# VectorE's steps on adaLN's columns behind the low part of the last piece but one, and the last turned x kept next to the first eviction

## The chip, the cores and the metric

The kernel runs on one core of a Trainium2 chip. The metric is the device time of one execution in microseconds (us). Three runs of the kernel before took 906.33, 906.44 and 906.9 us; the median, 906.44 us, is the time before.

## The reference, cut to what matters

Batch 1, 256 tokens, D = 2048, E = 4096, all in float32:

```python
h = rmsnorm(x, norm_g)
mod = einsum('bd,df->bf', silu(c), ada_w) + ada_b     # 2048 x 6144 weights
shift, scale, gate = split(mod, 3)
h = h * (1 + scale) + shift
proj = einsum('bsd,de->bse', h, w_in)                 # 2048 x 16384 weights
b_gate, c_gate, v, g = split(proj, 4)
u = causal_depthwise_conv(c_gate * v, conv_w)         # width 3
y = b_gate * u * silu(g)
x = x + gate * einsum('bse,ed->bsd', y, w_out)        # 4096 x 2048 weights
out = rmsnorm(x, final_g)
```

The first product needs h, h needs adaLN's scale and shift, and these are themselves products with 2048 x 4096 weights. What this change concerns is how the kernel works on both kinds of weights at the same time.

## The kernel before, in words

**Products in three parts.** A float32 weight tile is loaded as `raw_s`, cast by ScalarE to float32r as its high part `hi` (L352, `split_hi`), and VectorE subtracts that from `raw_s` and gets the low part `lo` (L357, `split_lo`). The tokens are held in the same way: `hT` has for each block k of 128 features a high and a low half. TensorE multiplies high by high, high by low and low by high (L491, `product`): three products of 128x256 for each block k and each 128 columns. The tiles `raw`, `hi` and `lo` have three buffers each; a load of two blocks takes half a tile, so that two such loads share one.

**adaLN in groups.** The 16 blocks of features are made ready in eight groups of two (`ADA`). The first group is made in a prologue written in a fixed order. For each later group eight pieces of `ada_w` are loaded as tiles `at` (L460, two loads of 256 KB each, four buffers), and VectorE adds them up, each multiplied by silu(c): one step for each of 16 rows into `gv` (L472 for the first, L474 for the others, in `ada_sums`, which is traced at a lower priority by `GIVE`). When a group's 16 steps are done, TensorE transposes the sums (`tp_g`, L481), VectorE reduces them (L482) and adds the biases (`mod`, L324), ScalarE writes the high tokens (`hT`, L328) and VectorE the low tokens (L332, L335). Only then may TensorE use these two blocks k.

**Pieces of w_in.** Sixteen outputs (4 column chunks by 4 quarters) share the first part of the program. `plan()` makes a list of steps from a table of costs: a piece of `ada_w`, or the products of one output with the blocks that are ready by then (`part`). In its list the first 13 outputs take the first two blocks only, and the next three the first four; later they come again for the rest. Each part ends with an eviction from PSUM (`keep`: ScalarE copies it at L512, or VectorE adds at L514). PSUM has three buffers for these.

**What sets the order.** Python traces the steps in the plan's order, and a scheduler then sorts every engine's instructions by data dependencies, priorities and its own estimate of times. An engine runs what it is given in that order. `tc.add_manual_dep` with `after` adds an order between two instructions of one engine without a semaphore; `in_order` ties the prologue so, and `behind(ended)` puts instructions behind the prologue's last one on their engine. `keep_x(3, tp_3)` moves the last four transposed blocks of x from PSUM to `xs3` by four ScalarE instructions (L317); before, it is traced behind the second eviction (L574 to L577).

**Names.** Numbers in the order's rows are those of the program's buffers: `hi_376` and `lo_377` are the parts of `raw_s_375`, whose two halves are two outputs' first two blocks. `hi_444` and `lo_445` belong to `raw_s_443`, the next such tile. `raw_s_747` (`hi_748`, `lo_749`, PSUM `mm_s_746`) is the first piece with four blocks, two of which belong to the second group; `raw_s_812` (`hi_813`, `lo_814`, `mm_s_811`) is the next, and `mm_s_710`, evicted to `acc31`, is the output ahead of both, `mm_s_658` (`acc20`) the one ahead of that, `mm_s_878` the one behind.

Of the kernel before, what the change touches and what calls it, by code (L numbers as in the profile page):

```python
# [8 lines left out]
F32 = mybir.dt.float32  # L9
F32R = mybir.dt.float32r  # L10
AF = mybir.ActivationFunctionType
ALU = mybir.AluOpType
# [105 lines left out]
def short_conv_layer(ctx: ExitStack, tc: tile.TileContext, x, c, norm_g, ada_w, ada_b, w_in, conv_w, w_out, final_g, out):  # L118
    nc = tc.nc
# [43 lines left out]
    after = mybir.DependencyInfo(mybir.DependencyClass.NoSync, mybir.DependencyReason.DATA)  # L163
# [14 lines left out]
    @contextmanager  # L178
    def behind(last):

        traced = nc.cur_bb.bb.instructions
        n = len(traced)
        yield
        for ins in list(traced[n:]):
            if ins.engine in last:
                tc.add_manual_dep(ins, last[ins.engine], after, reason="behind")
# [13 lines left out]
    ended = {}  # L200
# [113 lines left out]
    def keep_x(j, tp):  # L314
        for i in range(CT):
            k = j * CT + i
            nc.scalar.activation(xs[j][:, i], tp[:, i], AF.Copy, scale=gT[:, k : k + 1])  # L317
# [19 lines left out]
    def modulate(k0, nk, sums):  # L337

        add_biases(k0, nk, sums)
        for k in range(k0, k0 + nk):  # L340
            high_tokens(k)
            low_tokens(k)

    def hi_tile():
        return w_tile("hi", "hi", F32R)

# [7 lines left out]

    def split_lo(raw, n, hi, lo_tag="lo", lo=None):
        lo = lo_tile(lo_tag) if lo is None else lo
        nc.vector.tensor_tensor(out=lo[:, :n], in0=raw[:, :n], in1=hi[:, :n].bitcast(F32), op=ALU.subtract)  # L357
        return hi, lo

    HALF = SLOT // 2  # L360
# [36 lines left out]
    for k in range(KT):  # L397
        c_k = silu_c[:, k : k + 1]
        at, gv = first_ada[k], gv0
# [47 lines left out]
    acc = {}  # L447
# [19 lines left out]
    def ada_sums(j, kk, at4, gv):  # L467
        for i in range(kk):
            c_k = silu_c[:, j + i : j + i + 1]
            if j + i == 0:  # L470
                with behind(ended):
                    nc.vector.tensor_scalar_mul(gv, at4[:, i], c_k)  # L472
            else:
                nc.vector.scalar_tensor_tensor(out=gv, in0=at4[:, i], scalar=c_k, in1=gv, op0=ALU.mult, op1=ALU.add)  # L474

    def ada_done(k0, nk, gv):

# [19 lines left out]
    def chunk_products(bank, hi, lo, o0, k, k0, k1, seed=False, late=False):  # L497


        begins = k == k0 and not seed  # L500
        terms = [(m, i) for i in (0, 2, 1) for m in range(CT)] if late else [(m, i) for m in range(CT) for i in range(3)]
        for m, i in terms:
            o = slice(o0 + m * P, o0 + (m + 1) * P)
            product(bank[:, m, :], hi[:, o], lo[:, o], k, i, begins and i == 0, m % 2 == 0, k == k1 - 1 and (m, i) == terms[-1])
# [3 lines left out]
    def keep(ch, q, k0, bank, seed=False):  # L508
        if k0 == 0 or seed:
            if k0 == 0:  # L510
                acc[ch, q] = slot([P, CT, T], f"acc{ch}{q}")
            nc.scalar.copy(acc[ch, q], bank)  # L512
        else:
            nc.vector.tensor_tensor(out=acc[ch, q], in0=bank, in1=acc[ch, q], op=ALU.add)  # L514

    def part(ch, q, k0, k1, seed):


        col = q * E + ch * CT * P
        step = SLOT // (CT * P)  # L520
        first = k0
        bank = psum.tile([P, CT, T], F32, tag="mm", name="mm_s")
        if seed:
            nc.scalar.copy(bank, acc[ch, q])
        if pieces0:
            for k in range(NK0):
                chunk_products(bank, *pieces0[k], 0, k, k0, k1, late=True)
            pieces0.clear()
            k0 = NK0
        for s0 in range(k0, k1, step):  # L530
            sk = min(step, k1 - s0)
            n = sk * CT * P
            raw, hi, lo = places(n)
            nc.sync.dma_start(
                raw[:, :n].rearrange("p (k f) -> p k f", k=sk),
                w_in[0, s0 * P : (s0 + sk) * P, col : col + CT * P].rearrange("(k p) f -> p k f", p=P),
            )
            with behind(ended if len(acc) < 3 else {}):
                split_lo(raw, n, split_hi(raw, n, hi), lo=lo)
            for i in range(sk):  # L540
                chunk_products(bank, hi, lo, i * CT * P, s0 + i, k0, k1, seed)
        keep(ch, q, first, bank, seed)

    ys = []
# [16 lines left out]
    for kind, *step in plan():  # L561
        if kind == "ada":
            ada_piece(*step)
        else:
            ch, k1 = step[0], step[3]
            part(*step)
            if step[2] == 0 and len(acc) in LATER:
                with tc.issue_after(last_mm[0].ins), behind(ended):
                    if len(acc) == LATER[0]:
                        rows2 = rows_tile("rows2")  # L570
                        nc.sync.dma_start(rows2[:, :], conv_w.rearrange("w (k p) -> (w k) p", p=P))
                    else:
                        turn(rows2, 0, 96, cw)
            if tp_3 is not None and len(acc) == 2:  # L574
                with behind(ended):
                    keep_x(3, tp_3)
                tp_3 = None  # L577
            whole[ch] += k1 == KT
            if k1 == KT and whole[ch] == 4:
                mixed(ch)  # L580
# [311 lines left out]
```

## Time and profile before

| | |
|---|---|
| median of three runs | 906.44 us |
| the profiled execution's own time | 906.58 us |
| its span, first to last instruction | 904.8 us |
| TensorE (PE) busy | 890.3 us, 98% |
| VectorE (DVE) busy | 665.8 us, 74% |
| ScalarE (ACT) busy | 477.8 us, 53% |
| mean granted TensorE clock | 0.998 |

How to read the rows that follow: in the timeline's rows stand the start in us, the duration in us (of all of a row's instructions together), the engine, the line in the kernel, the operation, what it writes from what, the shape, and how many instructions the row merges; in square brackets how long the engine stood idle before it, and what ended that. In the stages' rows stand the stretch, its length, each engine's busy time (and instructions) in the order PE, PEld (weight loads), DVE, ACT, POOL, then the granted clock, the DMA engines' share and GB/s. SP is the engine that issues the loads.

### The profile page before, as it was taken

The numbers are of one execution on the slowest core, as the hardware profiler recorded it, in microseconds if no ns is written. First come the engines' busy times: TensorE is split into PE (matmuls) and PEld (weight loads), VectorE is DVE, ScalarE is ACT, GpSimd is POOL, SyncE is SP. The second block draws the span as 40 slices with busy tenths as digits, with TensorE's granted clock in tenths as the row PEclk, the third lists the DMA queues.
The fourth block names the chain that finished last, engine by engine and source line by source line (L and its number), as shares of the span: only waits on it lengthen the run. The fifth ranks groups of instructions, "written<-read, shape, count | busy, mean of one in ns | idle before, by whom it ended". The sixth has DMA issues, their size and how long they took to land.

```text
span 904.8 us, 16390 instructions
## 1 busy us (share of the span) xinstructions
PE 890.3 (98%) x7009; PEld 852.8 (94%) x7009; DVE 665.8 (74%) x643; ACT 477.8 (53%) x423; POOL 87.3 (10%) x95
## 2 busy tenths in 40 slices
PE   7999999999999999999999999999999999999996
PEld 4899999999999999999999999999999988888885
DVE  5889989888888866766965677565555578887882
ACT  6768866665548766644433444443444445544342
POOL 0000000000000134024324103420000000000000
PEclk9999999999999999999999999999999999999999
DMA  9999999999998587688887888776566486685542
GB/s 313 365 372 366 361 304 349 362 369 347 355 323 289 164 278 242 189 258 244 281 251 237 255 271 266 231 228 191 187 190 195 135 313 197 224 281 187 186 139 94
DMA packets 162665, 235.00 MB, mean 260 GB/s; under 512 B 6804, under 2 KB 105284, under 8 KB 162208
## 3 DMA queue, kind: packets, MB, share of 16 engines
q1 hardware_dynamic: 159456, 226.56, 76.4%
q0 software_dynamic: 3008, 7.34, 2.9%
q8 instruction: 55, 0.90, 0.4%
q14 instruction: 18, 0.15, 0.0%
q10 hardware_dynamic: 128, 0.04, 0.0%
HBM read 224.49 MB, written 2.10 MB: 250 GB/s over the span
## 4 chain that ended last, share of the span: by engine, by line
PE 94%; DMA 3%; SPq 1%; DVE 1%; issue 1%; ACT 0%; ACTq 0%; DVEq 0%
PE mm_b L491 38%; PE mm_s L491 36%; PE mm_o L724 10%; PE mm_w L724 7%; DMA at<-in_ada_w_dram 2%; PE mm L724 2%; SPq L231 1%; DMA x<-in_x_dram 1%; DVE lo L357 0%; PE tp_g L481 0%; ACT hi L352 0%; DVE gv L474 0%; DVE hT L335 0%; ACT big L817 0%; ACT z L866 0%
## 5 line engine op out<-in xcount | busy, mean ns | idle before, releaser
L491 PE MATMUL mm_s<-hT,hi 128*128 128x256 f32 x2048 | 350.0, 277 | 1.0 <-ACT hT L328 1.0
L491 PE MATMUL mm_b<-hT,hi 128*128 128x256 f32 x2048 | 348.2, 276 | 0.0
L491 PEld LDWEIGHTS mm_s<-hT,hi 128*128 128x128 f32 x2048 | 308.2, 188 | 1.2 <-ACT hT L328 1.2
L491 PEld LDWEIGHTS mm_b<-hT,hi 128*128 128x128 f32 x2048 | 308.6, 188 | 0.0
L491 PE MATMUL mm_s<-hT,lo 128*128 128x256 f32 x1024 | 282.3, 277 | 1.2 <-DVE lo L357 1.2
L491 PE MATMUL mm_b<-hT,lo 128*128 128x256 f32 x1024 | 282.6, 276 | 0.0
L357 DVE TENSOR_TENSOR lo<-raw,hi 128x2048 fp32r<-128x2048 f32 (+1 forms) x66 | 152.3, 2309 | 98.7 <-ACT hi L352 98.4
L352 ACT CAST hi<-raw 128x2048 fp32r<-128x2048 f32 (+1 forms) x66 | 123.7, 1875 | 190.7 <-PE mm_b L491 144.7
L491 PEld LDWEIGHTS mm_s<-hT,lo 128*128 128x128 f32 x1024 | 191.7, 188 | 1.8 <-DVE lo L357 1.8
L491 PEld LDWEIGHTS mm_b<-hT,lo 128*128 128x128 f32 x1024 | 192.2, 188 | 0.0
L357 DVE TENSOR_TENSOR lo<-raw_s,hi 128x2048 fp32r<-128x2048 f32 (+1 forms) x80 | 149.6, 1874 | 40.8 <-ACT hi L352 40.3
L352 ACT CAST hi<-raw_s 128x2048 fp32r<-128x2048 f32 (+1 forms) x80 | 124.1, 1558 | 58.6 <-PE mm_s L491 50.2
L352 ACT CAST hi<-raw_o 128x2048 fp32r<-128x2048 f32 x26 | 49.6, 1908 | 68.1 <-PE mm_o L724 36.6
L474 DVE SCALAR_TENSOR_TENSOR gv<-at,silu_c,gv 128x512 f32<-128x512 f32 x105 | 78.6, 749 | 4.4 <-DMA at<-in_ada_w_dram 2.7
L357 DVE TENSOR_TENSOR lo<-raw_o,hi 128x2048 fp32r<-128x2048 f32 x26 | 59.6, 2291 | 30.3 <-ACT hi L352 30.3
L724 PE MATMUL mm_o<-hi,y 128*128 128x512 f32 x256 | 78.6, 389 | 0.0
L512 ACT COPY acc<-mm_s 128x1024 f32<-128x1024 f32 x54 | 54.8, 1014 | 44.0 <-PE mm_s L491 43.8
L724 PE MATMUL mm_w<-hi,y 128*128 128x512 f32 x184 | 58.8, 389 | 0.0
L624 POOL TENSOR_TENSOR gacc<-gacc,z 128x512 f32<-128x512 f32 x28 | 47.4, 1692 | 115.2 <-DMA z<-gacc 115.2
L724 PEld LDWEIGHTS mm_o<-hi,y 128*128 128x128 f32 x256 | 48.0, 188 | 10.0
L618 DVE SCALAR_TENSOR_TENSOR gacc<-at_g,silu_c,gacc 128x512 f32<-128x512 f32 x60 | 48.0, 800 | 5.8 <-DMA at_g<-in_ada_w_dram 4.6
L724 PE MATMUL mm_o<-lo,y 128*128 128x512 f32 x128 | 49.5, 389 | 0.0
(145 smaller groups left out, 583.4 us busy)
## 6 DMA issues: line engine op xcount, KB each, us to landing
raw<-in_sc_w_in_dram SPq DMA_DIRECT2D x64, 1024.0 KB, 6.0
raw_s<-in_sc_w_in_dram SPq DMA_DIRECT2D x47, 1024.0 KB, 8.0
raw_o<-in_sc_w_out_dram SPq DMA_DIRECT2D x32, 1024.0 KB, 5.3
at<-in_ada_w_dram SPq DMA_DIRECT2D x114, 256.0 KB, 7.9
raw_s<-in_sc_w_in_dram SPq DMA_DIRECT2D x33, 512.0 KB, 7.1
at_g<-in_ada_w_dram SPq DMA_DIRECT2D x32, 512.0 KB, 8.4
at<-in_ada_w_dram SPq DMA_DIRECT2D x6, 512.0 KB, 9.4
x<-in_x_dram SPq DMA_DIRECT2D x4, 512.0 KB, 6.0
```

The source lines that it names most:

```text
L231: nc.sync.dma_start(at[:, :, s, :], adas[:, j : j + kk, s, 0 : NK0 * P])
L352: nc.scalar.copy(hi[:, :n], raw[:, :n])
L357: nc.vector.tensor_tensor(out=lo[:, :n], in0=raw[:, :n], in1=hi[:, :n].bitcast(F32), op=ALU.subtract)
L474: nc.vector.scalar_tensor_tensor(out=gv, in0=at4[:, i], scalar=c_k, in1=gv, op0=ALU.mult, op1=ALU.add)
L491: mm = last_mm[0] = nc.tensor.matmul(dst, w, h[k], start=begins and left, stop=ends, skip_group_check=True)
L512: nc.scalar.copy(acc[ch, q], bank)
L618: nc.vector.scalar_tensor_tensor(out=ga, in0=at3[:, i, :], scalar=s, in1=ga, op0=ALU.mult, op1=ALU.add)
L624: nc.gpsimd.tensor_tensor(out=ga, in0=ga, in1=turned, op=ALU.add)
L724: nc.tensor.matmul(dst, y[a], b, start=opens and i == 0, stop=ends and i == 2, skip_group_check=True)
```

## The change

Each low part's instruction name is kept in a list `lows`. Each step of `ada_sums` is then tied behind `lows[-2]`, the low part that was traced last but one ahead of it. `keep_x(3, tp_3)` is traced ahead of the first eviction instead of behind the second.

```diff
+    lows = []
...
     def split_lo(raw, n, hi, lo_tag="lo", lo=None):
         lo = lo_tile(lo_tag) if lo is None else lo
-        nc.vector.tensor_tensor(out=lo[:, :n], in0=raw[:, :n], in1=hi[:, :n].bitcast(F32), op=ALU.subtract)
+        low = nc.vector.tensor_tensor(out=lo[:, :n], in0=raw[:, :n], in1=hi[:, :n].bitcast(F32), op=ALU.subtract)
+        lows.append(low.ins.name)
         return hi, lo
...
             if j + i == 0:
                 with behind(ended):
-                    nc.vector.tensor_scalar_mul(gv, at4[:, i], c_k)
+                    step = nc.vector.tensor_scalar_mul(gv, at4[:, i], c_k)
             else:
-                nc.vector.scalar_tensor_tensor(out=gv, in0=at4[:, i], scalar=c_k, in1=gv, op0=ALU.mult, op1=ALU.add)
+                step = nc.vector.scalar_tensor_tensor(
+                    out=gv, in0=at4[:, i], scalar=c_k, in1=gv, op0=ALU.mult, op1=ALU.add
+                )
+            tc.add_manual_dep(step.ins, lows[-2], after, reason="low parts in the order of the loads")
...
+        if len(acc) == 1:
+            with behind(ended):
+                keep_x(3, tp_3)
         keep(ch, q, first, bank, seed)
...
-            if tp_3 is not None and len(acc) == 2:
-                with behind(ended):
-                    keep_x(3, tp_3)
-                tp_3 = None
```

The plan's steps are the same. The scheduler makes another order of them, on all engines, up to the end of the sixteen outputs; the number of instructions is the same. Line numbers shift: L352 is L354 in the changed kernel, L357 is L359, L460 is L463, L472 and L474 are L475 and L477, L481 is L487, L482 is L488, L491 is L497, L512 is L518.

First place, VectorE at the two halves of `lo_377`. Before:

```order
L357 TENSOR_TENSOR lo_377<-raw_s_375,hi_376 128x1024
L474 TENSOR_SCALAR gv_368<-at_407,silu_c_138,gv_368 128x512 x2
L474 TENSOR_SCALAR gv_368<-at_475,silu_c_138,gv_368 128x512 x2
L357 TENSOR_TENSOR lo_377<-raw_s_375,hi_376 128x1024
L474 TENSOR_SCALAR gv_368<-at_510,silu_c_138,gv_368 128x512 x2
L357 TENSOR_TENSOR lo_445<-raw_s_443,hi_444 128x1024 x2
```

And with the change:

```order
L477 TENSOR_SCALAR gv_368<-at_407,silu_c_138,gv_368 128x512
L359 TENSOR_TENSOR lo_377<-raw_s_375,hi_376 128x1024
L477 TENSOR_SCALAR gv_368<-at_407,silu_c_138,gv_368 128x512
L359 TENSOR_TENSOR lo_377<-raw_s_375,hi_376 128x1024
L477 TENSOR_SCALAR gv_368<-at_475,silu_c_138,gv_368 128x512 x2
L359 TENSOR_TENSOR lo_445<-raw_s_443,hi_444 128x1024
L477 TENSOR_SCALAR gv_368<-at_510,silu_c_138,gv_368 128x512
L359 TENSOR_TENSOR lo_445<-raw_s_443,hi_444 128x1024
```

The pair of steps on `at_475` has gone from ahead of the second half to behind it, and one step on `at_407` has come ahead of the first half. What TensorE runs there, in rows that are the same in both but for the line's number, is:

```order
L491 MATMUL mm_s_442<-hT_167,hi_444 128x256 x2
L491 MATMUL mm_s_480<-hT_167,hi_444 128x256 x2
L491 MATMUL mm_s_442<-hT_167,lo_445 128x256
L491 MATMUL mm_s_442<-hT_167,hi_444 128x256 x2
L491 MATMUL mm_s_442<-hT_167,lo_445 128x256
```

`mm_s_442` takes the first half of `hi_444`, `mm_s_480` the second; two products of the second half stand ahead of the first low part.

Second place, VectorE from the second group's reduction on. Before:

```order
L482 TENSOR_REDUCE gs_697<-tp_g_696 128x4
L324 TENSOR_TENSOR mod_173<-gs_697,vec_136 128x2x2
L472 TENSOR_SCALAR gv_740<-at_741,silu_c_138 128x512
L474 TENSOR_SCALAR gv_740<-at_741,silu_c_138,gv_740 128x512
L357 TENSOR_TENSOR lo_749<-raw_s_747,hi_748 128x2048
L474 TENSOR_SCALAR gv_740<-at_806,silu_c_138,gv_740 128x512
L332 TENSOR_SCALAR xs0_169<-xs0_169,mod_173 128x256 x2
L474 TENSOR_SCALAR gv_740<-at_806,silu_c_138,gv_740 128x512
L335 TENSOR_TENSOR hT_167<-xs0_169,hT_167 128x256 x2
L474 TENSOR_SCALAR gv_740<-at_868,silu_c_138,gv_740 128x512 x2
L357 TENSOR_TENSOR lo_814<-raw_s_812,hi_813 128x2048
```

And with the change:

```order
L488 TENSOR_REDUCE gs_697<-tp_g_696 128x4
L359 TENSOR_TENSOR lo_749<-raw_s_747,hi_748 128x2048
L477 TENSOR_SCALAR gv_740<-at_806,silu_c_138,gv_740 128x512
L324 TENSOR_TENSOR mod_173<-gs_697,vec_136 128x2x2
L477 TENSOR_SCALAR gv_740<-at_806,silu_c_138,gv_740 128x512
L477 TENSOR_SCALAR gv_740<-at_868,silu_c_138,gv_740 128x512
L359 TENSOR_TENSOR lo_814<-raw_s_812,hi_813 128x2048
L477 TENSOR_SCALAR gv_740<-at_868,silu_c_138,gv_740 128x512
L332 TENSOR_SCALAR xs0_169<-xs0_169,mod_173 128x256 x2
```

`mod` has gone behind `lo_749` and a step on `gv`, and the low tokens (L332, L335) behind `lo_814`. ScalarE at the same place, before:

```order
L352 COPY hi_748<-raw_s_747 128x2048
L328 ACTIVATE hT_167<-xs0_169,mod_173 128x256 x2
L512 COPY acc20_689<-mm_s_658 128x1024
L512 COPY acc31_738<-mm_s_710 128x1024
L352 COPY hi_813<-raw_s_812 128x2048
```

And with the change:

```order
L354 COPY hi_748<-raw_s_747 128x2048
L518 COPY acc20_689<-mm_s_658 128x1024
L518 COPY acc31_738<-mm_s_710 128x1024
L354 COPY hi_813<-raw_s_812 128x2048
L328 ACTIVATE hT_167<-xs0_169,mod_173 128x256 x2
```

The second group's two casts to `hT` stand behind the cast of `hi_813`.

Third place, TensorE at these two pieces, behind the first 24 products of `mm_s_746` (its first two blocks), which are the same in both. Before, its other 24 products come next; then:

```order
L250 MATMUL tp_v_803<-ident_127,rows2_621 128x96
L491 MATMUL mm_s_811<-hT_167,hi_813 128x256 x2
L491 MATMUL mm_s_811<-hT_167,lo_814 128x256
L491 MATMUL mm_s_811<-hT_167,hi_813 128x256 x2
L491 MATMUL mm_s_811<-hT_167,lo_814 128x256
```

With the change the 24 are followed by:

```order
L497 MATMUL mm_s_811<-hT_167,hi_813 128x256 x2
L497 MATMUL mm_s_746<-hT_167,hi_748 128x256
L497 MATMUL mm_s_811<-hT_167,lo_814 128x256
L497 MATMUL mm_s_811<-hT_167,hi_813 128x256 x2
L497 MATMUL mm_s_811<-hT_167,lo_814 128x256
```

The other products of `mm_s_746` come later between those of `mm_s_811`, so that `lo_814`'s first product stands behind 27 products of these two pieces instead of 51 (with `tp_v`, the transpose of the convolution's weights); from it to the last of both 70 are left instead of 46.

On SP the order of the loads is the same up to `at_583`; from there some loads of `raw_s` change places with pairs of loads of `at`, `raw_s_812` coming ahead of the two loads of `at_868`.

## The prediction

> **What bounds the kernel now.** I read the page's head and busy times first, then TensorE's waits between 25 and 740 us, then the pace of its products in the chain that ended last.
>
> ```profile
> span 904.8 us, 16390 instructions
> PE 890.3 (98%) x7009; PEld 852.8 (94%) x7009; DVE 665.8 (74%) x643; ACT 477.8 (53%) x423; POOL 87.3 (10%) x95
> ```
>
> ```profile
> PE mm_s L491 <- DVE lo L357: 1.2, 2, 0.9
> PE mm_s L491 <- ACT hT L328: 1.0, 1, 1.0
> ```
>
> ```profile
> 378.98 348.16 PE mm_b L491 x3072
> ```
>
> The reader sees a TensorE that is busy 98% of the span. Of its waits after the first products only two lie where this change works, both for a low part (L357), one near 36 us and one near 68 us; the wait for hT stands at the very first product, ahead of everything the change moves. A product of 256 columns costs 348.16/3072 = 0.113 us when nothing is waited for; that is the exchange rate below. TensorE's work does not change, so the question is only how long it stands still between 25 and 80 us.
>
> The **first wait** in TensorE's, VectorE's and ScalarE's rows, one fence for each, and the load at that time:
>
> ```profile
> 36.15 0.39 PE L491 MATMUL mm_s<-hT,hi 128*128 128x256 f32 x2
> 37.41 0.39 PE L491 MATMUL mm_s<-hT,lo 128*128 128x256 f32 x1 [0.88 <-DVE lo L357]
> ...
> 40.05 0.62 PE L491 MATMUL mm_s<-hT,hi 128*128 128x256 f32 x4
> ```
>
> ```profile
> 32.38 1.53 DVE L474 SCALAR_TENSOR_TENSOR gv<-at,silu_c,gv 128x512 f32<-128x512 f32 x2
> 34.69 1.54 DVE L474 SCALAR_TENSOR_TENSOR gv<-at,silu_c,gv 128x512 f32<-128x512 f32 x2 [0.78 <-DMA at<-in_ada_w_dram]
> 36.14 1.22 DVE L357 TENSOR_TENSOR lo<-raw_s,hi 128x1024 fp32r<-128x1024 f32 x1
> ```
>
> ```profile
> 33.45 1.07 ACT L352 CAST hi<-raw_s 128x1024 fp32r<-128x1024 f32 x1
> ...
> 37.65 1.05 ACT L352 CAST hi<-raw_s 128x1024 fp32r<-128x1024 f32 x1 [0.29 <-DMA raw_s<-in_sc_w_in_dram]
> 38.95 1.05 ACT L352 CAST hi<-raw_s 128x1024 fp32r<-128x1024 f32 x1 [0.25 <-DMA raw_s<-in_sc_w_in_dram]
> ```
>
> ```profile
> 27.00:41.00 14.00, 13.06 (x113) 12.66 (x112) 12.04 (x14) 10.90 (x14) 0.00 (x0) 1.00 1.07 367
> ```
>
> The cast of the second half of raw_s_375 was done at 33.45 + 1.07 = 34.52, but its low part started at 36.14: VectorE stood 0.78 us waiting for a piece of adaLN's columns, then ran two steps on it, with the low part behind them. Without the wait TensorE's third product would have come at 36.15 + 2 x 0.113 = 36.38, not 37.41. **1.03 us are lost there.**
>
> The **second wait**, in the same three engines' rows:
>
> ```profile
> 55.82 0.60 PE L481 MATMUL tp_g<-ident,gv 128*128 128x128 f32 x4
> ...
> 62.31 0.39 PE L491 MATMUL mm_s<-hT,hi 128*128 128x256 f32 x2
> ...
> 67.78 0.48 PE L491 MATMUL mm_s<-hT,hi 128*128 128x256 f32 x2
> 68.55 0.39 PE L491 MATMUL mm_s<-hT,lo 128*128 128x256 f32 x1 [0.29 <-DVE lo L357]
> ```
>
> ```profile
> 57.96 1.92 ACT L352 CAST hi<-raw_s 128x2048 fp32r<-128x2048 f32 x1
> 59.77 1.09 ACT L328 ACTIVATE hT<-xs,mod 128x256 fp32r<-128x256 f32 x2
> ...
> 62.51 1.02 ACT L512 COPY acc<-mm_s 128x1024 f32<-128x1024 f32 x1 [0.74 <-PE mm_s L491]
> 63.42 1.92 ACT L352 CAST hi<-raw_s 128x2048 fp32r<-128x2048 f32 x1
> ```
>
> ```profile
> 57.71 0.16 DVE L324 TENSOR_TENSOR mod<-gs,vec 128x4 f32<-128x4 f32 x1
> ...
> 59.91 2.29 DVE L357 TENSOR_TENSOR lo<-raw_s,hi 128x2048 fp32r<-128x2048 f32 x1 [0.84 <-ACT hi L352]
> ...
> 64.76 1.53 DVE L474 SCALAR_TENSOR_TENSOR gv<-at,silu_c,gv 128x512 f32<-128x512 f32 x2
> 66.21 2.29 DVE L357 TENSOR_TENSOR lo<-raw_s,hi 128x2048 fp32r<-128x2048 f32 x1
> ```
>
> TensorE came to lo_814 at 67.78 + 0.23 = 68.01 and got it at 68.55: **0.54 us.** The whole prize of putting low parts first is 1.03 + 0.54 = 1.57 us, 0.17% of the time.
>
> **The change part by part.** It adds no instruction; it moves steps on VectorE, casts on ScalarE, loads on SP and, through the scheduler, products on TensorE.
>
> *Four casts of keep_x(3).* 1.58 us of ScalarE (row below) go from behind the second eviction to behind the first.
>
> ```profile
> 27.84 1.02 ACT L512 COPY acc<-mm_s 128x1024 f32<-128x1024 f32 x1
> 30.15 1.05 ACT L352 CAST hi<-raw_s 128x1024 fp32r<-128x1024 f32 x1 [1.30 <-DMA raw_s<-in_sc_w_in_dram]
> ...
> 32.01 1.58 ACT L317 ACTIVATE xs<-tp_x,vec 128x256 f32<-128x256 f32 x4
> ```
>
> They fill the 1.30 us in which ScalarE waited for raw_s_375: 27.84 + 1.02 + 1.58 = 30.44 at the latest, so that cast is at most 0.3 us later. The cast of the second half can come sooner, since it no longer stands behind them. I cost this at nothing; the cover is the wait below.
>
> *First wait.* In the new order only one step on at_407 stands between the two halves, and the pair on at_475 comes behind. That at_407 step now precedes the first half's low part; it has landed by 32.38 at the latest, so that low part ends by 32.38 + 0.77 + 1.22 = 34.4 and the second by 36.4 even then, near enough to its need at 36.38. The stall goes, and TensorE comes to the next piece at 40.05 - 1.03 = 39.02. **What is late next is the load.** The order of TensorE there is unchanged: two products with hi_444's first half, then one with its second half. That half's cast waited for its DMA until 38.95 and ended at 40.00; SP's order up to that load is the same, and the load ran at 367 GB/s with a DMA share of 1.07, so nothing can bring it sooner. TensorE goes on at 40.00 + 0.05 = 40.05 (0.05 is the step from a low part's end, 36.14 + 1.22, to 37.41); before, it was at that product at 40.05 + 0.23 = 40.28. **Gain: 0.23 us, of the 1.03.** Bounds: 0 (a wakeup as late as before) and 1.03 (the load comes as much sooner as TensorE). I take 0.23, since two rows fix it.
>
> *Second place.* Here the low parts come ahead of adaLN's work, and that work is on the path. The sums' transposes (tp_g) stand 30 products (3.4 us) further on than at 55.82, the reduction follows them, lo_749 (2.29 us) is ahead of mod, and one step on gv more. On ScalarE the two hT casts have gone from ahead of acc20 to behind hi_813. So the second half of piece 746 has no hT until hi_813 is cast, and the scheduler has put 811's first products, lo_814's among them, ahead of it. From the last product of 710, at 62.31 - 0.23 = 62.08, the chain is: acc31 copied from 62.51 - 0.23 = 62.28, hi_813 cast from 63.42 - 0.23 = 63.19 to 65.11, lo_814 from 65.14 to 67.43 (0.03 behind the cast as at 57.96 + 1.92 to 59.91), its product at 67.48. In this time TensorE has 24 products of 746, two of 811 and one more of 746: 27 x 0.113 = 3.05 of 5.40 us. **It stands still for about 2.3 us.** It is 67.48 - 68.55 = 1.07 us ahead of before at that product, but 24 products of the pair of pieces (2.72 us) are still to do that before had behind it: 70 then, against 46. **Net: 2.72 - 1.07 = 1.65 us later, with the 0.23 already in it.**
>
> hi_813's own load now comes two loads sooner on SP, which brings nothing: its cast at 63.42 stood behind the copy, not behind its DMA. The steps on gv that are later on VectorE are wanted only for the next transposes. POOL has nothing in this stretch (0.00 in the stage's row).
>
> Bounds of the second place: -0.54 (the stall simply goes) and, if nothing overlaps, 2.29 + 0.77 for a low part and a gv step more in the chain, +3.1. I take the chain, since each of its links has a row.
>
> [...]
>
> *The sum.* The profiled execution took 906.58 us (its span of 904.8 and 1.8 around it). 906.58 + 1.65 = 908.23. The median of the runs, 906.44, lies 0.14 below it, so I predict **908.1 us**, 0.18% more. From 80 us on TensorE has no listed wait until 740, so nothing gives the delay back. A difference of about 0.2% (1.81 us) is what a measurement of this kernel can tell from no change; the forecast lies just within.
>
> **The rivals.**
> *The change does what it says* and both stalls go: 906.44 - 1.57 = 904.9. For it: the low parts do come sooner. Against: the cast row at 38.95 ends on a DMA, and hT is behind hi_813 in the new order. 7%.
> *The first gain lasts*: TensorE stays 1.03 ahead, not 0.23, so the second chain starts 0.80 sooner: 906.44 + 0.85 = 907.3. It needs raw_s_443's second half by 37.9; the saturated load speaks against it. 9%.
> *Slower by more: hT is late for a further group too.* The next group has the same pattern in the new order, a 128x2048 low part ahead of mod. It decides if TensorE comes to that group's first product before hT's cast; the price is up to 2.29 a time, so 906.44 + 1.65 + 2.29 = 910.4, or part of it. For it: VectorE is busy 19.83 of 20 us from 60 to 80 (row below) and must run late. Against: TensorE lists no wait for any later group before. 17%.
>
> ```profile
> 60.00:80.00 20.00, 19.71 (x173) 19.51 (x173) 19.83 (x24) 13.85 (x14) 0.00 (x0) 1.00 1.07 369
> ```
>
> **How the numbers follow.** The forecast, +1.2 to +2.1 us, has 67%: 45 of it within 0.2% and 22 above, since 1.65 is so near 1.81. With the last rival's 17 that makes slower 39%. Same: 45, the 9, and 5 of the first rival's 7, 59%; faster 2%, as the whole prize is 0.17%. The range leaves out the first rival and the larger half of the last: 906.9 to 909.5, whose upper end is the second place's bound of 3.1.
>
> **What would show it.** Right: TensorE's wait near 36 us gone, and a new one of about 0.8 us near 39 for a cast hi (ACT L354), with its cast ended on the DMA; tp_g near 55.82 + 3.4 = 59.2; two short waits near 65 (hi, hT) and one of near 2 us for lo_814 until about 67.5; every product behind that pair of pieces about 1.65 us later than before, by the same distance to the end. Wrong: no wait near 39, or hT's casts ahead of hi_813 in time, or a wait of TensorE between 80 and 700.

## The result, and the profile after

The changed kernel took 909.84 us (median of 8 runs, 907.73 to 910.22), the kernel before 906.47 (8 runs, 905.93 to 906.9). The ratio is 1.0031, with an interval of 1.0022 to 1.0041: it is slower by 2.0 to 3.7 us. Its runs are not one heap but two: three at a mean granted clock of 0.998 (907.73, 908.25, 908.61) and five at 0.996 (909.56 to 910.22). The execution profiled below is of the first group, 908.25 us; the forecast's sum for a profiled execution was 908.23.

TensorE's waits between 25 and 740 us in the changed kernel (engine, line, releaser: us in total, times, longest), after the head of its page. The head counts 10 instructions fewer than before (16380 against 16390); those that do work are as many as before on each engine:

```profile
span 906.5 us, 16380 instructions
PE 890.1 (98%) x7009; PEld 852.9 (94%) x7009; DVE 662.7 (73%) x643; ACT 477.1 (53%) x423; POOL 87.7 (10%) x95
```

```profile
PE mm_s L497 <- DVE lo L359: 1.4, 1, 1.4
PE mm_s L497 <- ACT hT L328: 1.0, 1, 1.0
PE mm_s L497 <- ACT hi L354: 0.6, 1, 0.6
```

The old wait near 37 is gone and a wait for a cast has come; the old wait for `lo_814`, 0.29 us, has become one of 1.44. The first place, in the rows of TensorE and ScalarE:

```profile
39.87 0.51 PE L497 MATMUL mm_s<-hT,hi 128*128 128x256 f32 x2 [0.59 <-ACT hi L354]
```

```profile
38.77 1.05 ACT L354 CAST hi<-raw_s 128x1024 fp32r<-128x1024 f32 x1 [0.24 <-DMA raw_s<-in_sc_w_in_dram]
```

The wait of 0.88 us near 37 has become one of 0.59 us near 39, for the second half of the next load, and the cast that it waits for began when its DMA had landed. The second place, in the rows of TensorE, ScalarE and VectorE:

```profile
58.62 0.60 PE L487 MATMUL tp_g<-ident,gv 128*128 128x128 f32 x4
...
64.72 0.28 PE L497 MATMUL mm_s<-hT,lo 128*128 128x256 f32 x1
65.12 0.88 PE L497 MATMUL mm_s<-hT,hi 128*128 128x256 f32 x3
67.45 0.38 PE L497 MATMUL mm_s<-hT,lo 128*128 128x256 f32 x1 [1.44 <-DVE lo L359]
```

```profile
62.25 1.02 ACT L518 COPY acc<-mm_s 128x1024 f32<-128x1024 f32 x1 [1.74 <-PE mm_s L497]
63.16 1.91 ACT L354 CAST hi<-raw_s 128x2048 fp32r<-128x2048 f32 x1
64.97 1.09 ACT L328 ACTIVATE hT<-xs,mod 128x256 fp32r<-128x256 f32 x2
```

```profile
59.86 2.28 DVE L359 TENSOR_TENSOR lo<-raw_s,hi 128x2048 fp32r<-128x2048 f32 x1
62.73 0.15 DVE L324 TENSOR_TENSOR mod<-gs,vec 128x4 f32<-128x4 f32 x1
65.10 2.29 DVE L359 TENSOR_TENSOR lo<-raw_s,hi 128x2048 fp32r<-128x2048 f32 x1 [0.72 <-ACT hi L354]
```

The hT casts (L328) stand behind the cast hi of 63.16, the low part follows that cast, and its product comes at 67.45. Between 65.00 and 67.45 TensorE did only three products, 0.34 us of work: it stood still for 2.1 us. In the chain that ended last (start, us, what) the products behind it follow without a gap:

```profile
67.45 6.31 PE mm_s L497 x53
...
380.58 348.16 PE mm_b L497 x3072
```

The products of mm_b begin at 380.58, against 378.98 before, and take the same 348.16. No wait of TensorE is listed between 80 and 740. So the profile explains 1.60 us, and with it the first group of runs; the other five runs took 1.9 us more, and that this profile doesn't show.

### The profile page after: what moved, and what is told of

It is laid out like the page before. It is cut to its first block, busy times and chain, and to the rows that moved or that the text cites. A ratio compares the mean times of both kernels' runs of the same rounds, so it can differ in the third digit from the quotient of the medians.

```text
span 906.5 us, 16380 instructions
## 1 busy us (share of the span) xinstructions
PE 890.1 (98%) x7009; PEld 852.9 (94%) x7009; DVE 662.7 (73%) x643; ACT 477.1 (53%) x423; POOL 87.7 (10%) x95
## 4 chain that ended last, share of the span: by engine, by line
PE 94%; DMA 3%; SPq 1%; ACT 1%; DVE 0%; issue 0%; ACTq 0%
PE mm_b L497 38%; PE mm_s L497 37%; PE mm_o L729 10%; PE mm_w L729 7%; PE mm L729 2%; DMA at<-in_ada_w_dram 2%; DMA raw_s<-in_sc_w_in_dram 1%; SPq L231 1%; DMA x<-in_x_dram 1%; PE tp_g L487 0%; ACT hi L354 0%; DVE lo L359 0%; SPq L463 0%; SPq L540 0%; ACT big L822 0%
## 5 line engine op out<-in xcount | busy, mean ns | idle before, releaser
L497 PE MATMUL mm_s<-hT,hi 128*128 128x256 f32 x2048 | 350.8, 277 | 1.7 <-ACT hT L328 1.0
L497 PE MATMUL mm_b<-hT,hi 128*128 128x256 f32 x2048 | 348.2, 276 | 0.0
L497 PEld LDWEIGHTS mm_s<-hT,hi 128*128 128x128 f32 x2048 | 308.6, 188 | 2.5 <-ACT hT L328 1.4
L497 PEld LDWEIGHTS mm_b<-hT,hi 128*128 128x128 f32 x2048 | 308.3, 188 | 0.0
L497 PE MATMUL mm_s<-hT,lo 128*128 128x256 f32 x1024 | 282.0, 277 | 1.5 <-DVE lo L359 1.4
L497 PE MATMUL mm_b<-hT,lo 128*128 128x256 f32 x1024 | 282.6, 276 | 0.0
L359 DVE TENSOR_TENSOR lo<-raw,hi 128x2048 fp32r<-128x2048 f32 (+1 forms) x66 | 152.9, 2318 | 100.5 <-ACT hi L354 100.2
L354 ACT CAST hi<-raw 128x2048 fp32r<-128x2048 f32 (+1 forms) x66 | 123.7, 1875 | 192.5 <-PE mm_b L497 146.9
L497 PEld LDWEIGHTS mm_s<-hT,lo 128*128 128x128 f32 x1024 | 191.7, 188 | 1.9 <-DVE lo L359 1.9
L497 PEld LDWEIGHTS mm_b<-hT,lo 128*128 128x128 f32 x1024 | 192.2, 188 | 0.0
L359 DVE TENSOR_TENSOR lo<-raw_s,hi 128x2048 fp32r<-128x2048 f32 (+1 forms) x80 | 149.8, 1877 | 46.6 <-ACT hi L354 46.2
L354 ACT CAST hi<-raw_s 128x2048 fp32r<-128x2048 f32 (+1 forms) x80 | 124.0, 1557 | 88.8 <-PE mm_s L497 74.0
L354 ACT CAST hi<-raw_o 128x2048 fp32r<-128x2048 f32 x26 | 49.6, 1908 | 68.0 <-PE mm_o L729 36.6
L359 DVE TENSOR_TENSOR lo<-raw_o,hi 128x2048 fp32r<-128x2048 f32 x26 | 59.5, 2289 | 30.2 <-ACT hi L354 30.2
L477 DVE SCALAR_TENSOR_TENSOR gv<-at,silu_c,gv 128x512 f32<-128x512 f32 x105 | 78.2, 747 | 3.1 <-DMA at<-in_ada_w_dram 1.9
L518 ACT COPY acc<-mm_s 128x1024 f32<-128x1024 f32 x54 | 54.4, 1011 | 20.0 <-PE mm_s L497 19.9
L627 POOL DMA_DIRECT2D z<-gacc x28 | 15.7, 561 | 350.9 <-DVE acc L564 286.8
```

What stands on the lines that cost most here:

```text
L354: nc.scalar.copy(hi[:, :n], raw[:, :n])
L359: low = nc.vector.tensor_tensor(out=lo[:, :n], in0=raw[:, :n], in1=hi[:, :n].bitcast(F32), op=ALU.subtract)
L477: step = nc.vector.scalar_tensor_tensor(out=gv, in0=at4[:, i], scalar=c_k, in1=gv, op0=ALU.mult, op1=ALU.add)
L497: mm = last_mm[0] = nc.tensor.matmul(dst, w, h[k], start=begins and left, stop=ends, skip_group_check=True)
L627: nc.gpsimd.dma_start(turned[0 : P - away], ga[away:P])
```

## The experiments

Theory 1 says that the order alone makes the loss, and that the second group is scatter. Theory 2 says that standing still near 65 us is in some executions followed by a stretch at a lower granted clock (the granted clock is the share of its full speed that TensorE was given, as the profile records it). Rival 3 puts the loss, or part of it, on the four casts of keep_x(3) that were moved. All runs, by the mean granted clock of each (n runs, median, lowest to highest):

| kernel | TensorE's wait in question | at 0.997 to 0.999 | at 0.996 or less |
|---|---|---|---|
| changed | 1.44 us, 2.1 with the products between | 3: 908.25 (907.73–908.61) | 5: 910.13 (909.56–910.22) |
| again | the same | 4: 908.45 (908.38–908.83) | 3: 909.82 (909.34–910.16) |
| lows_only | the same | 2: 907.77 (907.76–907.77) | 4: 909.96 (909.65–910.19) |
| tie_first4 | the same | 2: 908.67 (908.3–909.03) | 4: 910.10 (909.5–910.24) |
| keep_only | none at the second place | 11: 906.27 (905.71–906.77) | 0 |
| tie_first3 | none at the second place | 11: 906.16 (905.68–906.67) | 0 |
| gap1 | none (nothing was held up) | 11: 906.67 (906.09–907.07) | 0 |
| gap2 | none (nothing was held up) | 11: 906.64 (906.02–907.01) | 0 |
| gap2_busy | none, 4.5 us of added products | 5: 910.99 (910.36–912.96) | 0 |
| stand2 | 1.25 us, put in | 12: 908.22 (907.55–908.64) | 0 |
| stand3 | 1.73 us, put in | 8: 908.82 (908.03–909.03) | 0 |
| stand4 | 2.21 us, put in | 3: 908.5, 909.55, 910.86 | 3: 911.18 (910.48–911.28) |
| stand6 | 3.16 us, put in | 1: 910.88 | 4: 911.46 (911.03–912.63) |

The kernel before ran beside them with medians of 906.67 (beside again, keep_only, lows_only and tie_first3), 906.62 (beside tie_first4 and the gaps), 906.62 (beside stand2 and stand4) and 906.52 (beside stand3 and stand6), and not one of its runs compared was at 0.996. One of them, beside stand2 and stand4, took 909.68 at 0.997: a late time without a lower mean clock is possible.

### The changed kernel again

No edit.

> The changed kernel once more, unaltered. Its first eight runs fell into two groups: 907.73 to 908.61 us at a mean granted clock of 0.998, and 909.56 to 910.22 at 0.996. Theory 1 (order alone): TensorE stands still for about 2.3 us near 65 us and is 1.6 us late from there on; the second group is scatter of the measurement and its profile, if one is caught, shows the same stages at the same clock with some transfer late: then no clock below 1.00 between 30 and 890 us. Theory 2 (order and clock): the standing still is sometimes followed by a stretch of a few us at a lower granted clock, worth the other 1.9 us (0.002 of 908 is 1.8). Then again two groups near 908.2 and 910.1, at 0.998 and 0.996, and a profile of the second group shows the granted clock under 1.00 somewhere behind 65 us and the products in it at up to twice 0.113 us, with everything else as in the first profile.

Measured: two groups again, 1.0027 of before (1.0015 to 1.0038). The profile taken was once more of the first group, with mm_b begun at 380.59 and the same waits. The groups repeat, so they are no accident of one session; what makes the second was still open.

### One part alone: the casts of the last turned x

The edit, against the kernel before:

```diff
+        if len(acc) == 1:
+            with behind(ended):
+                keep_x(3, tp_3)
         keep(ch, q, first, bank, seed)
...
-            if tp_3 is not None and len(acc) == 2:
-                with behind(ended):
-                    keep_x(3, tp_3)
-                tp_3 = None
```

> Kernel before, with only one part of the change: the casts of the last turned x (keep_x(3)) behind the first eviction; no order is put on VectorE's steps. Theories 1 and 2 both put the whole loss on the order of the low parts: here sums and hT casts stay as before at the second place, so 906.0 to 906.4 us, one group of runs at 0.998, no wait for lo near 67. If the second half of the cast of raw_s_375 is free sooner, the wait of 0.88 us near 37 goes too and a wait for the cast of the next load near 39 takes its place: 0.2 to 0.4 us of gain. Rival 3 (the moved casts cost: they delay the cast of raw_s_375 and TensorE stands still behind it): 907 us or more with a wait of TensorE for hi between 29 and 34.

Measured: 906.27 us, 0.9995 of before (0.9986 to 1.0004), one group. Of TensorE's waits only one in the stretch is left, and VectorE shows why the old one near 37 is gone:

```profile
39.95 0.51 PE L491 MATMUL mm_s<-hT,hi 128*128 128x256 f32 x2 [0.63 <-ACT hi L352]
```

```profile
33.41 0.74 DVE L474 SCALAR_TENSOR_TENSOR gv<-at,silu_c,gv 128x512 f32<-128x512 f32 x1
34.08 1.22 DVE L357 TENSOR_TENSOR lo<-raw_s,hi 128x1024 fp32r<-128x1024 f32 x1
```

The low part that came at 36.14 in the kernel before comes at 34.08, with no order put on VectorE by hand; the scheduler itself has put it behind one step on gv. So the moved casts are enough to remove the first wait, the next load takes its place as forecast, and rival 3 falls. TensorE's wait for `lo_814` near 68 is gone here too.

### The other part alone: the order of the low parts

The edit, against the changed kernel: the casts are put back.

```diff
-        if len(acc) == 1:
-            with behind(ended):
-                keep_x(3, tp_3)
...
+            if tp_3 is not None and len(acc) == 2:
+                with behind(ended):
+                    keep_x(3, tp_3)
+                tp_3 = None
```

> The other part alone: VectorE's steps on gv are put behind the low part of the last piece but one, the casts of the last turned x stay behind the second eviction. Theory 1: as the changed kernel, TensorE's products for lo_814 near 67.5 after about 2 us of waiting, 908.2 us in all runs. Theory 2: two groups of runs as the changed kernel has them, near 908.2 at 0.998 and 910.1 at 0.996. Rival 3: within 0.5 us of before, one group.

Measured: 909.74 us, 1.0029 of before (1.0017 to 1.0041), in two groups, with the wait of 1.4 us for a low part as the only one listed between 26 and 740 us. The whole loss, both of its parts, belongs to the order of the low parts.

### Which of the ordered steps costs

tie_first3 and tie_first4 are one number apart. Against the changed kernel, with 6 in tie_first3 and 8 in tie_first4:

```diff
-            tc.add_manual_dep(step.ins, lows[-2], after, reason="low parts in the order of the loads")
+            if len(sums) == 1 and j < 6:
+                tc.add_manual_dep(step.ins, lows[-2], after, reason="low parts in the order of the loads")
```

> The changed kernel, but the order is put only on the steps on gv of the first group's first three pieces (two steps each); the fourth piece's and all later groups' steps are free. The first wait near 37 should go as in the changed kernel. If what costs at the second place is that the fourth piece's steps (from the tile at_510) come behind the low part there, so that the sums' end, and with it mod and hT, slip behind lo and hi of the next pieces, then here the second place is as before: no wait of 2 us for lo_814, 906.0 to 906.4 us, one group at 0.998. If any such order on VectorE costs it, as much as the changed kernel: 908 to 910.

> As tie_first3, with one piece more: the order is put on the steps on gv of the first group's first four pieces, the two steps from at_510 among them, and on no others. If the fourth piece's order is what flips the second place, these two steps bring back all of the loss: a wait of TensorE of 1.4 us and more for lo_814 near 67, products of mm_b begun near 380.6, runs near 907.8 to 908.4 at a clock of 0.998, and, if the clock theory holds, others near 909.6 to 910.2 at 0.996. If the loss needs the order of the later groups as well, it is as tie_first3: 905.7 to 906.7.

Measured: tie_first3 906.16 us, 0.9995 of before (0.9986 to 1.0003), one group; tie_first4 909.76, 1.0032 (1.0021 to 1.0044), two groups. The tie of two steps on VectorE decides it. No wait of TensorE is listed in tie_first3 between 26 and 740 us. VectorE's rows there:

```profile
56.30 0.68 DVE L489 TENSOR_REDUCE gs<-tp_g 128x4 f32<-128x512 f32 x1
57.02 0.16 DVE L324 TENSOR_TENSOR mod<-gs,vec 128x4 f32<-128x4 f32 x1
...
59.20 2.29 DVE L359 TENSOR_TENSOR lo<-raw_s,hi 128x2048 fp32r<-128x2048 f32 x1 [0.77 <-ACT hi L354]
```

and in tie_first4:

```profile
59.24 0.69 DVE L489 TENSOR_REDUCE gs<-tp_g 128x4 f32<-128x512 f32 x1 [0.37 <-PE tp_g L488]
59.85 2.28 DVE L359 TENSOR_TENSOR lo<-raw_s,hi 128x2048 fp32r<-128x2048 f32 x1
62.05 0.74 DVE L477 SCALAR_TENSOR_TENSOR gv<-at,silu_c,gv 128x512 f32<-128x512 f32 x1
62.71 0.16 DVE L324 TENSOR_TENSOR mod<-gs,vec 128x4 f32<-128x4 f32 x1
```

The reduction of the sums is 2.94 us later, so the low part of 2.3 us goes ahead of mod, mod is 5.69 us later, and the hT casts that read it fall from ahead of the next cast hi to behind it. On ScalarE, first tie_first3, then tie_first4:

```profile
59.06 1.09 ACT L328 ACTIVATE hT<-xs,mod 128x256 fp32r<-128x256 f32 x2
...
62.70 1.92 ACT L354 CAST hi<-raw_s 128x2048 fp32r<-128x2048 f32 x1
```

```profile
63.13 1.91 ACT L354 CAST hi<-raw_s 128x2048 fp32r<-128x2048 f32 x1
64.94 1.09 ACT L328 ACTIVATE hT<-xs,mod 128x256 fp32r<-128x256 f32 x2
```

### The clock, seen

The execution of tie_first4 that was profiled took 910.19 us, at 0.996: the second group at last. Its stages around the wait (busy us and count of each engine, then the granted clock, the DMA share and GB/s), and TensorE's rows behind it:

```profile
62.00:68.00 6.00, 4.45 (x33) 3.85 (x32) 5.26 (x8) 5.71 (x5) 0.00 (x0) 1.00 1.07 367
68.00:71.00 3.00, 3.00 (x17) 3.00 (x15) 3.00 (x7) 0.00 (x0) 0.00 (x0) 0.50 1.07 371
71.00:75.00 4.00, 4.00 (x35) 4.00 (x35) 2.63 (x3) 0.00 (x0) 0.00 (x0) 0.95 1.08 377
75.00:80.00 5.00, 5.00 (x47) 5.00 (x46) 4.51 (x6) 4.67 (x5) 0.00 (x0) 1.00 0.93 314
```

```profile
67.42 0.39 PE L498 MATMUL mm_s<-hT,lo 128*128 128x256 f32 x1 [1.45 <-DVE lo L359]
67.65 0.39 PE L498 MATMUL mm_s<-hT,hi 128*128 128x256 f32 x2
67.88 0.33 PE L498 MATMUL mm_s<-hT,lo 128*128 128x256 f32 x1
68.01 0.63 PE L498 MATMUL mm_s<-hT,hi 128*128 128x256 f32 x2
68.44 0.41 PE L498 MATMUL mm_s<-hT,lo 128*128 128x256 f32 x1
...
71.21 0.48 PE L498 MATMUL mm_s<-hT,hi 128*128 128x256 f32 x2
71.53 0.28 PE L498 MATMUL mm_s<-hT,lo 128*128 128x256 f32 x1
```

Up to the product at 67.42 the execution is that of the changed kernel (67.45). Then the granted clock is 0.50, and from 68.01 to 68.44 two products take 0.43, 0.215 us each instead of 0.113; near 71.4 it is back at 1.00. The profile's record of the clock gives this stretch as 3.413 us, so half of it, 1.7 us, is lost. In the chain that ended last it is to be seen in the 53 products that took 6.31 us above:

```profile
67.42 7.94 PE mm_s L498 x53
```

7.94 - 6.31 is 1.63 us, and up to the start of mm_b nothing else differs (382.22 against 380.58). This is in the range of the differences between the two groups (1.4 to 2.2 us by the medians of the table).

### Standing still without a changed order

What remained was whether the standing still or something else in the new order halves the clock. The next kernels leave the order of before as it is and hold TensorE up near 700 us, with additions on GpSimd that nothing else uses. The first pair held nothing up. Against the kernel before, with two additions of 128x128 in gap1 and four in gap2:

```diff
+    def stand():
+        for n in STAND:
+            op = nc.gpsimd.tensor_tensor(out=rest[:, :n], in0=rest[:, :n], in1=rest[:, :n], op=ALU.add)
+            tc.add_manual_dep(op.ins, over[0] or last_mm[0].ins.name, after, reason="one behind the other")
+            over[0] = op.ins.name
+    def held(mm):
+        if over[0]:
+            tc.add_manual_dep(mm.ins, over[0], after, reason="TensorE stands")
...
+                            held(last_mm[0])
+                            if (ct, q, kp, m, i, j) == (NCT - 2, QUARTERS[1], 0, 1, 2, 2):
+                                stand()
```

> Kernel before, its order on TensorE, VectorE, ScalarE and SP the same to the last instruction; but near 700 us, between two products of mm_b, TensorE waits for two added instructions of GpSimd, one behind the other, which TensorE's wait covers in full. An estimate from the rows of GpSimd's additions (1692 ns for 128x512, 905 for 128x256) gives some 1.0 us of standing still. Theory 1 (the second group of runs is not caused by standing still): before + 1.0, one group. Theory 2 (a stretch of a lower clock follows standing still of a certain length): at 1.0 us also one group at 0.998 if it is too short, since the kernel before stands still for 0.88 us near 37 and has one group.

> As gap1 with four additions, some 2.1 us of standing still, as long as that of the changed kernel near 65 us, but in one piece and with no change of any order. Theory 2: a part of the runs at a mean clock of 0.996 and 1.6 to 1.9 us longer than the rest, which lie near before + 2.1, 908.7; a profile in the longer group shows the granted clock under 1.00 behind the standing still. Theory 1: one group near 908.7 at 0.998; then the second group of the changed kernel comes from something else in its order.

Measured: 906.67 and 906.64 us, 0.9999 (0.999 to 1.0008) and 1.0 (0.9991 to 1.0009). The dependence `after` made no engine wait for another here: GpSimd did its additions 100 us early, and no wait of TensorE for them is listed. The row of gap1's additions (shortest, median and longest ns, first and last start):

```profile
L662 POOL TENSOR_TENSOR rest<-rest x2: 455/494/532, 597.3 to 597.8; 128x128 f32<-128x128 f32 x2
```

So these two say nothing of standing still. They show how far apart runs of one order lie (below).

> The control of gap2: at the same place TensorE does five added products of 512 columns on constants, which no result uses, where gap2 lets it wait. By the rows of ten such products at the start (4.58 us) they cost some 2.2 us. Theory 2: as late as gap2's shorter group, near 908.7, in one group at 0.998, since TensorE never stands still. If two groups come here as well, it is the delay and not the standing still that makes them.

The edit puts, in place of GpSimd's additions, five products of 512 columns on constants between the same two products. Measured: 910.99 us, 1.0047 of before (1.0033 to 1.0061), all five runs at 0.998 or 0.999. They cost twice what I expected: each is recorded as two rows.

```profile
L660 PE MATMUL tp_fill<-ones,ident 128*128 128x512 f32 x10 | 4.5, 592 | 0.0
```

906.62 + 4.5 is 911.1. The profiled execution, 912.96, lost more in a wait of 1.5 us for a low part near 538, whose chain goes back to a load of adaLN's columns that took 11.23 us at 509, long before the edit's place. A delay of 4.5 us in which TensorE was busy left the clock alone: none of the five runs is at 0.996.

The mended kernels wait for GpSimd in earnest; they differ in the number of additions, which their names give. The first addition waits for a product, the next product for the last addition, and all later products are put behind that one. Against gap2:

```diff
-    over = [None]
+    over = [None, None]
+    waits = mybir.DependencyInfo(mybir.DependencyClass.Sync, mybir.DependencyReason.DATA)
...
-            tc.add_manual_dep(op.ins, over[0] or last_mm[0].ins.name, after, reason="one behind the other")
+            if over[0] is None:
+                tc.add_manual_dep(op.ins, last_mm[0].ins.name, waits, reason="GpSimd begins")
...
-        if over[0]:
-            tc.add_manual_dep(mm.ins, over[0], after, reason="TensorE stands")
+        if over[0] and over[1] is None:
+            tc.add_manual_dep(mm.ins, over[0], waits, reason="TensorE stands")
+            over[1] = mm.ins.name
+        elif over[1]:
+            tc.add_manual_dep(mm.ins, over[1], after, reason="behind it")
```

> gap1 and gap2 mended: there TensorE's products were only put in order behind GpSimd's additions, which began at 597 us and held nobody up, so neither said anything of standing still. Here the first addition waits for a product of mm_b near 700 us, and the next product for the last addition. Two additions of 494 ns with the wakeups: some 1.2 us of standing still. The profile of tie_first4 shows the granted clock at 0.50 from about 67.8 to 71.2 us, right behind the standing still, at 0.214 us a product instead of 0.113. Theory 2, with numbers now: the clock is granted anew for stretches of 3.41 us, at random phase to the program, and halved for one when TensorE was busy for less than about half of the stretch before. Then 1.2 us never halves it: one group, before + 1.2 = 907.8, at 0.998. Theory 1 (the halving comes of something else in the changed order): one group as well.

> As stand2 with four additions: some 2.3 us of standing still, with no change of any order. Theory 2: of stretches of 3.41 us at random phase, one holds more than 1.7 us of the 2.3 in 2.3/3.41 = 67% of the executions; so about two thirds of the runs near before + 2.3 + 1.7 = 910.6 at a clock of 0.996, the rest near 908.9 at 0.998, nothing between but by chance. Theory 1: all runs near 908.9 at 0.998.

> As stand4 with three additions. stand2 and stand4 showed waits of 1.25 and 2.21 us for two and four, so some 1.7 to 1.75 us here, close to half of a stretch (3.413/2 = 1.71). If the bound is half a stretch, this is the shortest wait that can halve the clock: with the bound just below, 50% of the executions in a longer group near before + 1.75 + 1.7 = 910.1 at 0.996; with it just above, all near 908.4 at 0.998. If the bound is lower (1.3 us would still let stand2 pass), (3.41 + 1.75 - 2.6)/3.41 = 75% in the longer group.

> As stand4 with six additions: some 3.15 us of standing still, still shorter than one stretch of 3.41. By a bound of half a stretch 3.15/3.41 = 92% of the executions lose 1.7 us more: nearly all near before + 3.15 + 1.7 = 911.5 at 0.996, hardly one near 909.8. If only a whole stretch of standing still halved the clock, none would.

The wait in each, in the order stand2, stand3, stand4, stand6:

```profile
699.45 0.50 PE L491 MATMUL mm_b<-hT,hi 128*128 128x256 f32 x2 [1.25 <-POOL rest L663]
```

```profile
700.09 0.50 PE L491 MATMUL mm_b<-hT,hi 128*128 128x256 f32 x2 [1.73 <-POOL rest L663]
```

```profile
700.25 0.50 PE L491 MATMUL mm_b<-hT,hi 128*128 128x256 f32 x2 [2.21 <-POOL rest L663]
```

```profile
701.06 0.50 PE L491 MATMUL mm_b<-hT,hi 128*128 128x256 f32 x2 [3.16 <-POOL rest L663]
```

Measured: with 1.25 us none of 12 runs, with 1.73 none of 8, with 2.21 three of 6 at 0.996, with 3.16 four of 5 at 0.996 or less. (In each of the last two, one more run at 0.997 was late, 910.86 and 910.88; whether its clock was halved the mean doesn't show.) The ratios to before are 1.0015 (1.0006 to 1.0023), 1.0025 (1.0014 to 1.0036), 1.0037 (1.0024 to 1.005) and 1.0056 (1.0043 to 1.0069). Behind the 2.21 us the clock was halved, in the profiled execution for 3.413 us by its record, which two stages show:

```profile
702.00:705.00 3.00, 3.00 (x19) 3.00 (x19) 0.00 (x0) 1.79 (x1) 0.00 (x0) 0.63 0.45 159
...
706.00:712.00 6.00, 6.00 (x56) 6.00 (x55) 2.97 (x3) 2.72 (x3) 0.00 (x0) 1.00 0.54 176
```

19 products in 3 us, and at the full clock 56 in 6. The chain that ended last has the price, in the 255 products from this wait to the end of mm_b, for stand3 and for stand4:

```profile
700.09 29.22 PE mm_b L491 x255
```

```profile
700.25 30.80 PE mm_b L491 x255
```

1.58 us more, with the same order everywhere; stand6 has the same 30.80 from its 701.06 on. Theory 1 falls: standing still did it by itself, without the changed order, at 2.21 and 3.16 us and not at 1.25 and 1.73.

That the bound is half a stretch (1.71 us) these counts neither show nor exclude: stand4 had 3 of 6 where 67% were expected, stand6 4 of 5 where 92% were, and stand3 lay on the bound. The profiles' records of the clock say more. Every stretch in them but the last, which the end cuts off, is a whole number of 3.413 us long: 17 before the halving in tie_first4, 203 in stand4, 261 in the kernel before. So the bounds can be counted back from the fall of the clock near the end of each execution, also where nothing was halved. At 0.113 us a product a stretch has room for the starts of 30 products (3.413/0.113). How many began in the stretch in which TensorE stood still most near 67 or near 700 us, and the clock granted in the next:

| execution | that stretch | products begun | clock in the next |
|---|---|---|---|
| stand6 | 698.08 to 701.49 | 3 | 0.50 |
| stand4 | 697.41 to 700.82 | 8 | 0.50 |
| tie_first4 | 64.56 to 67.98 | 9 | 0.50 |
| lows_only | 64.78 to 68.19 | 12 | 1.00 |
| stand3 | 696.57 to 699.98 | 14 | 1.00 |
| again | 65.78 to 69.19 | 15 | 1.00 |
| stand2 | 696.32 to 699.73 | 17 | 1.00 |
| changed | 62.94 to 66.36 | 19 | 1.00 |

In these eight profiles it is how much of the wait falls into one stretch that goes with the halving: in the changed kernel's profile a bound at 66.36 cuts the standing still in two. The limit lies between 9 and 12 of 30 products in them, which is below the half that theory 2 assumed. How the chip measures idleness they don't show.

## Why the prediction was right, and what it lacked

*The first place* went as forecast in its waits. The wait near 37 is gone, and the cast that TensorE now waits for began behind its DMA (0.24 us in its row). The wait is 0.59 us, not 0.8. The moved casts are enough for it: keep_only has it without the order that was meant to bring it. Whether the order is enough by itself stays open: lows_only has no wait near 37 either, but its loads came 0.87 us sooner than before's (30.02 against 30.89).

*The gain of 0.23 us there* is too small to be read from two profiles, and at equal loads it isn't there. The group of loads of raw_s to which that half belongs was begun by SP between 30.38 and 31.10 us in the executions that have the order of before, and mm_b began the later, the later it was:

| execution (order of before) | first load of that group issued at | mm_b begins at |
|---|---|---|
| gap2 | 30.38 | 378.31 |
| gap1 | 30.47 | 378.47 |
| stand6 | 30.65 | 378.64 |
| stand4 | 30.78 | 378.79 |
| stand2 | 30.87 | 378.94 |
| kernel before | 30.89 | 378.98 |
| stand3 | 31.07 | 379.10 |
| gap2_busy | 31.10 | 379.14 |

The changed kernel's profile has 30.73 and 380.58; a kernel before with that issue time lies near 378.73. So the order costs 1.85 us at equal loads. The medians of the runs at 0.997 and above say the same: 908.25 - 906.47 and 908.45 - 906.67 are both 1.78. The forecast was 1.65. The difference is about the 0.23: the 211th product into mm_s, between the two places, starts at 50.26 in the kernel before, at 50.00 in the changed kernel, but at 49.92 in stand6, which has the order of before and loads issued 0.08 us sooner than the changed kernel. So being ahead there was the loads' doing.

*The second place* was right link by link: acc copied at 62.25 (forecast 62.28), hi cast from 63.16 (63.19), the low part from 65.10 (65.14), its product at 67.45 (67.48). TensorE stood still for 2.1 us (2.3). That the times agree to 0.03 us is in part luck: each of them has the 0.23 in it, which the early loads of this execution supplied. tp_g came at 58.62, not 59.2: in the trace it stands 27 products further on than before, not 30. Products that were ready behind the wait did not fill it: those with hi_813, cast by 65.07, went on only at 67.67, behind the low part's at 67.45, as those with hi_376, cast by 34.52, went on only at 37.64 in the kernel before, behind its wait of 0.88 us.

*The rivals.* That the change does what it says fell with the wait at 39 and the one at 67. That the first gain lasts fell with the DMA in the row of 38.77. That hT is late for a further group fell too: no wait is listed from 80 to 740. Its 910.4 is near what five runs took (909.56 to 910.22), but that is a coincidence: they took it by another mechanism.

*The step that failed* is the exchange rate behind the wait. The prediction says that "the question is only how long it stands still", and "every product behind that pair of pieces about 1.65 us later than before, by the same distance to the end" takes 0.113 us a product for granted after the standing still. In 16 of the 27 runs of the four kernels with this wait the mean clock was 0.996 or less: the profiled one of them had its clock halved for 3.413 us and lost 1.63 us by it; that the others did too is inferred from their mean clocks and times. So a term of its own was missing, 1.7 us in about 6 of 10 executions. With five of eight runs in that group the median went to 909.84, 0.34 above the range's end (by the ratio, 906.44 x 1.0031 = 909.25, it is inside); the forecast of 908.1 is that of the other group. That the range comes so near is luck: its upper end was worked out from a low part and a step on gv in the chain, not from the clock. The profile of before could hardly have shown it: its waits here, 0.88 and 0.29 us, are both below the 1.73 that did nothing.

## What to carry to other kernels

An order put on an engine to serve one wait moves what is tied behind it (here the reduction by 2.94 us, and mod by 5.69): look for the short instruction on the path (here mod, 0.16 us) that falls behind a long one (here a low part, 2.28), and follow it to the casts that read it. Price a standing still of TensorE of about 2 us or more (here 1.73 did nothing in 8 runs, and 2.21 was followed by a lower mean clock in three of 6, 3.16 in four of 5) not only by its length but by a stretch at half the clock behind it (here 3.413 us), in a part of the executions; count waits together when only a few products lie between them (here three between 65.00 and 67.45). When runs of a kernel come in two groups, compare their granted clocks first. The two parts of a change belong in separate kernels: here one alone takes both old waits away (906.27 against 906.67, less than these runs can tell from nothing), the other alone brings all of the loss.

## What the runs showed of the hardware

*The clock.* After 2.1 to 3.2 us of standing still TensorE's granted clock was 0.50 for 3.413 us in three profiled executions, in both places (near 68 and near 701), and a product took 0.215 us instead of 0.113 (two in 0.43 from 68.01 in tie_first4, from 701.26 in stand4 and from 701.50 in stand6). In the eight profiles of the table it came when 9 products or fewer of 30 had begun in the stretch before, and not with 12 or more. 1.25 and 1.73 us did nothing in 20 runs, 4.5 us of delay with TensorE busy nothing in 5. With the low parts in the changed order the bounds of the stretches fall at 62.94, 65.78 and 64.78 us (changed, again and lows_only), so they do not keep to one time of the program. A standing still of 2.21 us, shorter than one stretch, was enough in three of six runs.

*The loads at the start.* With one and the same order, the issue of a group of loads near 30 us differs by 0.7 us between eight profiled executions (30.38 to 31.10), and the start of mm_b by 0.8 with it (378.31 to 379.14). That is more than the 0.23 us that the first place was to bring, and it may be most of the 1 us by which the eight runs of the kernel before differ; what sets the issue these runs don't show.
